# A two-layer hybrid encoder trunk on one core: the feed-forward up phase is ordered by a planner in the source, its first two pairs of tiles are interleaved, and the output projection ahead of it runs tile by tile

## The chip, the core and the metric

One core of a Trainium2 chip. The engines named below are PE (matmuls; PEld is its weight load), DVE (vector), ACT (activations), POOL (GpSimd) and SP, which only issues transfers here. The metric is the time of one launch on the device in microseconds (us); lower is better.

## What is computed

Two layers on x of 1024 tokens by 1024 channels, float32. Layer 0 mixes tokens by grouped-query attention, layer 1 by multi-scale pooling; each layer then cross-attends into 256 memory tokens and runs a gated feed-forward part. The change lies where cross-attention ends and the feed-forward part begins:

```python
x = x + memory_cross_attention(...)        # ends in  o @ w_o, 1024 x 1024
x = x + conv_gated_ffn(rmsnorm(x, ffn_norm[i]), ...)

def conv_gated_ffn(h, w_up, conv_w, conv_b, w_down):
    u = h @ w_up                            # 1024 -> 2 * 2816
    up = jnp.pad(u, ((0, 0), (1, 1), (0, 0)))
    u = up[:, :-2] * conv_w[0] + up[:, 1:-1] * conv_w[1] + up[:, 2:] * conv_w[2] + conv_b
    gate, val = u[..., :D_FF], u[..., D_FF:]
    return (jax.nn.silu(gate) * val) @ w_down
```

## The kernel before

Float32 accuracy is had from three matmuls per product. Each operand is split into a rounded high part and a low remainder by `hi_lo` (line 150: ACT writes the high part at L153, DVE the remainder at L154), and `mm3` (lines 230 to 235) multiplies high by high, high by low and low by high. Operands live in 20 slots `R` of 128x2048, handed out whole or by halves, the longest-free one first. Float32 staging tiles `scr` are six buffers of 128x1024. PSUM has two tiles `pA` of 128x1024 and four `pB` of 128x512. The residual stream is eight tiles `X` of 128 tokens by 1024 channels.

**The output projection.** `project` (lines 248 to 273) runs over the two column halves n of w_o, and in each over the eight token tiles t, with 24 matmuls a tile, and adds the result into X (L261). In the second half the RMS norm of a tile follows its add (`first`, L723 and L219; the old X goes to DRAM as `Xd` before the norm overwrites it), and one tile later its transposes (`second`, L718).

**The up-projection by seven products.** For each of the 22 pairs f (a gate block and a value block of 128 columns of w_up) the product of a 2x2 block matrix of weights A by a 2x2 block matrix of transposed tokens B is taken by seven block products in place of eight. The rows of A are gate and value, its columns the lower and upper 512 channels; the columns of B are two groups of four token tiles, here tiles 0 to 3 and 4 to 7. Token side: `seven_into` (lines 706 to 748) makes B11, B21, B22 and the sums T1 = B12 - B11, T2 = B22 - T1, T3 = B22 - B12, T4 = B21 - T2. It takes the differences in the row layout, on DVE and POOL (L733), and transposes every one of the seven operands of each tile pair by itself. T3 and T4 are left to `tail` (lines 743 to 747), after the projection. Weight side: `load` (L771) brings a gate and a value block, each 512 KB with 128 columns a row, into two of four tiles; `sums` (lines 779 to 785) makes S1 to S4 on POOL into the other two; `split` gives the seven operands to `hi_lo`. Each product is 12 matmuls. Products that share a bank accumulate into it after it has been read: bank z takes P1, P6, P7 and P4 in turn, bank y takes P5 and P3, and P2 has a bank of its own; each product's result is read out before the bank's next one, by a copy on ACT (L811, L879, L882, L896) or an add on DVE (L817, L885, L890).

**The loop.** `ffn_main` (lines 831 to 912) runs the pairs one after the other in the order P1, P5, P6, P3, P7, P2 of the next pair, P4, with one split of the next pair after each product. The weights of pair f+2 and their sums follow at the end of pair f. Then come the convolution (`conv`: one ACT pass at L841, two DVE passes at L842 and L843), the gate's SiLU (L887), the product of gate and value (L902) and the store to the DRAM tile `G` (L903). From pair 1 on, the four weight tiles of a pair are tiles of X, which are free once their transposed forms have been split: pair 1 has X4 to X7. The instruction order of this stage is that of the framework's scheduler. After the last pair, `operand` (line 849) brings rows of G and of w_down back and splits them, and `down` (line 914) multiplies in rounds of four f.

Of the kernel before, what the change touches and what calls it, by code (L numbers as in the profile page):

```python
# [10 lines left out]
F32 = mybir.dt.float32  # L11
# [5 lines left out]
P = 128  # L17
# [98 lines left out]

class Kernel:
# [29 lines left out]
    def stat(self, n, name):  # L147
        return self.st.tile([P, n], F32, name=name, bufs=4)

# [472 lines left out]
    def cross(self, i, hT, qT, ws):  # L622
# [19 lines left out]
        def scores(t):  # L642
# [19 lines left out]
            if t % 4 == 3:  # L662
                for h in range(XH):
                    R.put(qT[h, half])

        def turn(t):
            if t % 4 == 0:
                PT[t // 4] = [R.get() for _ in range(4)]
            self.transposed(prs.pop(t), self.put_T(PT[t // 4], t))
# [17 lines left out]
        for t in range(4):  # L687
            scores(t)
# [5 lines left out]
        turn(4)  # L694
        values(0, (2, 3))
        turn(5)
        turn(6)
# [8 lines left out]
    def seven_into(self, X, gain, Xd):  # L706

        nc, R = self.nc, self.R  # L710
        H = {}

        def turn(name, t, src):
            if name not in H:
                H[name] = [R.get(), R.get()]
            p = self.psB().rearrange("p (a b) -> p a b", a=4)
            for k in range(4):
                nc.tensor.transpose(p[:, k, :], src[:, k * P:(k + 1) * P], self.ident)  # L718
            h, l = (R.v(s, 4)[:, :, (t % 4) * P:(t % 4 + 1) * P] for s in H[name])
            self.hi_lo(h, l, p)  # L720

        def first(t):
            nc.sync.dma_start(out=Xd[t * P:(t + 1) * P, :], in_=X[t])  # L723
            self.normed(X[t], gain, X[t])

        def second(t):
            lo, hi = slice(0, 512), slice(512, 1024)
            if t < 4:
                turn("B11", t, X[t][:, lo])
                turn("B21", t, X[t][:, hi])  # L730
                return
            x, y = X[t - 4], X[t]
            sub = lambda e, out, p, q: e.tensor_tensor(out=out, in0=p, in1=q, op=OP.subtract)  # L733
            sub(nc.vector, x[:, lo], y[:, lo], x[:, lo])
            t2 = self.extra
            sub(nc.vector, t2, y[:, hi], x[:, lo])
            sub(nc.gpsimd, y[:, lo], y[:, hi], y[:, lo])
            sub(nc.gpsimd, x[:, hi], x[:, hi], t2)
            turn("B22", t, y[:, hi])
            turn("T1", t, x[:, lo])  # L740
            turn("T2", t, t2)
# [6 lines left out]
        return (first, second), H, tail  # L748

    def ffn(self, i, H, X, Xd):  # L750
        nc, R, a = self.nc, self.R, self.a
# [4 lines left out]
        cp = self.psB()[:, :4 * 2 * NF].rearrange("p (j f) -> p j f", j=4)  # L756
        for j in range(4):
            nc.tensor.transpose(cp[:, j, :], c3[:, j, :], self.ident[:2 * NF, :2 * NF])
        cv = self.cst.tile([P, 4, 2 * NF], F32, name="conv")
        nc.vector.tensor_copy(cv, cp)  # L760
        wu, wd = a["ffn_w_up"][i], a["ffn_w_down"][i]
        G = self.tc.dram_tile([FF, S], F32, name=f"G{i}")
        raws, ops, bank = {}, {}, {}
        spare = []

        def load(f):

            tiles = [spare.pop(0) for _ in range(4)] if spare else [self.scr() for _ in range(4)]
            for j, c in ((0, f), (1, NF + f)):
                src = wu[:, c * P:(c + 1) * P].rearrange("(k p) n -> p k n", p=P)  # L770
                nc.sync.dma_start(out=tiles[j].rearrange("p (k n) -> p k n", k=NK), in_=src)  # L771
            raws[f] = tiles

        def blocks(f):
            g, v, s, u = raws[f]
            return {"A11": g[:, :512], "A12": g[:, 512:], "A21": v[:, :512], "A22": v[:, 512:],
                    "S1": s[:, :512], "S2": s[:, 512:], "S3": u[:, :512], "S4": u[:, 512:]}

        def sums(f):
            b = blocks(f)  # L780
            tt = nc.gpsimd.tensor_tensor
            tt(out=b["S1"], in0=b["A21"], in1=b["A22"], op=OP.add)  # L782
            tt(out=b["S2"], in0=b["S1"], in1=b["A11"], op=OP.subtract)
            tt(out=b["S4"], in0=b["A12"], in1=b["S2"], op=OP.subtract)
            tt(out=b["S3"], in0=b["A11"], in1=b["A21"], op=OP.subtract)

        def halves(h):
            return R.hv(h)[:, :512], R.hv(h)[:, 512:]

        def split(f, name):  # L790
            h = ops[f, name] = R.get_half()
            self.hi_lo(*halves(h), blocks(f)[name])

        def done(f):
            if f:
                spare.extend(raws[f])
            del raws[f]

        def product(f, left, right, out, start):

            ah, al = (x.rearrange("p (k n) -> p k n", k=4) for x in halves(ops[f, left]))
            bh, bl = (R.v(s, 4) for s in H[right])
            for k in range(4):
                self.mm3(out, ah[:, k], al[:, k], bh[:, k], bl[:, k], start and k == 0, k == 3, not start)
            R.put_half(ops.pop((f, left)))

        def p2(f):
            x = self.psB()
            product(f, "A12", "B21", x, True)
            u = bank[f] = {"g": self.scr()}  # L810
            nc.scalar.copy(u["g"][:, :512], x)  # L811

        def p1(f):
            u = bank[f]
            z = u["z"] = self.psB()
            product(f, "A11", "B11", z, True)
            nc.vector.tensor_tensor(out=u["g"][:, :512], in0=z, in1=u["g"][:, :512], op=OP.add)  # L817

        load(0)
        sums(0)  # L820
        for n in ("A12", "A11", "S1", "S2"):
            split(0, n)

        def go():
            p2(0)
            p1(0)

        return go, lambda late, tail: self.ffn_main(H, X, Xd, late, tail, cv, G, wd, spare, load, sums, split, done,
                                                    product, p1, p2, bank)

    def ffn_main(self, H, X, Xd, late, tail, cv, G, wd, spare, load, sums, split, done, product, p1, p2, bank):
        nc, R = self.nc, self.R
        tail()
        for n in ("S4", "S3", "A22"):
            split(0, n)
        done(0)
        spare.extend(X[t] for t in (4, 5, 6, 7, 0, 1, 2, 3))

        def conv(u, f):
            c = self.scr()  # L840
            nc.scalar.activation(c, u, AF.Identity, scale=cv[:, 1, f:f + 1], bias=cv[:, 3, f:f + 1])  # L841
            nc.vector.scalar_tensor_tensor(c[:, 1:], u[:, :S - 1], cv[:, 0, f:f + 1], c[:, 1:], op0=OP.mult, op1=OP.add)  # L842
            nc.vector.scalar_tensor_tensor(c[:, :S - 1], u[:, 1:], cv[:, 2, f:f + 1], c[:, :S - 1], op0=OP.mult, op1=OP.add)  # L843
            return c

        rounds = [list(range(f, min(f + 4, NF))) for f in range(0, NF, 4)]
        hl = {}

        def operand(kind, f):

            raw = self.scr()
            nc.sync.dma_start(out=raw, in_=(G if kind == "g" else wd)[f * P:(f + 1) * P, :])
            hs = hl[kind, f] = [R.get_half(), R.get_half()]
            self.hi_lo(R.hv(hs[0]), R.hv(hs[1]), raw)

        first = [(kind, f) for f in rounds[0] for kind in ("g", "d")]
        order = ("A12", "A11", "S1", "S2", "S4", "S3", "A22")
        load(1)
        sums(1)
        for f in range(NF):  # L860
            u, left = bank[f], list(order)

            def ahead(n=1):
                for _ in range(n):
                    if f + 1 < NF:
                        if left:
                            split(f + 1, left.pop(0))
                            if not left:
                                done(f + 1)
                    elif first:  # L870
                        operand(*first.pop(0))
# [274 lines left out]
```

## Time and profile before

| | |
|---|---|
| median of 3 runs | 2660.0 us (2659.31 to 2660.57) |
| the profiled execution, its own time | 2661.13 us |
| its span, first to last instruction | 2659.4 us |
| granted TensorE clock, mean | 0.992 |
| HBM read and written | 166.42 MB and 35.65 MB |

The span is what the trace shows; the execution's own time has 1.7 us more around it. In the trace layer 0's output projection runs from about 845 to 949 us, its up phase to about 1381 us and its down phase to about 1600 us; in layer 1 the same stretches lie at about 1875 to 1978, to 2410 and to 2630 us. "PE busy" counts a matmul from its start to its modelled end; since matmuls overlap, what a stage costs is read better from the number of matmuls in a window and the distance between their starts.

### The profile page before, as it was taken

The numbers are of one execution on the slowest core, as the hardware profiler recorded it, in microseconds if no ns is written. First come the engines' busy times: TensorE is split into PE (matmuls) and PEld (weight loads), VectorE is DVE, ScalarE is ACT, GpSimd is POOL, SyncE is SP. The second block draws the span as 40 slices with busy tenths as digits, with TensorE's granted clock in tenths as the row PEclk, the third lists the DMA queues.
The fourth block names the chain that finished last, engine by engine and source line by source line (L and its number), as shares of the span: only waits on it lengthen the run. The fifth ranks groups of instructions, "written<-read, shape, count | busy, mean of one in ns | idle before, by whom it ended". The sixth has DMA issues, their size and how long they took to land.

```text
span 2659.4 us, 36296 instructions
## 1 busy us (share of the span) xinstructions
PE 2595.0 (98%) x13913; PEld 2216.8 (83%) x13913; DVE 1720.5 (65%) x2291; ACT 1207.8 (45%) x2024; POOL 695.0 (26%) x709
## 2 busy tenths in 40 slices
PE   8989999999999999999999998999999999999998
PEld 7988888888898878888878888889878888887886
DVE  6779999955246387777765435425378777767434
ACT  4448888843135255454542205425245555444111
POOL 3664445521012153433300001102034333310001
PEclk9999999999999999999999999999999999999999
DMA  4200000032222132223254203322122232326201
GB/s 157 83 1 1 1 1 1 2 135 65 70 80 89 48 95 73 94 72 95 87 187 154 100 19 89 103 64 72 58 92 91 72 95 72 95 104 241 99 24 63
DMA packets 167554, 209.22 MB, mean 79 GB/s; under 512 B 6741, under 2 KB 134077, under 8 KB 167381
## 3 DMA queue, kind: packets, MB, share of 16 engines
q1 hardware_dynamic: 167381, 206.91, 23.4%
q8 instruction: 109, 1.79, 0.3%
q14 instruction: 64, 0.52, 0.1%
HBM read 166.42 MB, written 35.65 MB: 76 GB/s over the span
## 4 chain that ended last, share of the span: by engine, by line
PE 57%; DVE 2%; ACT 2%; DMA 1%; issue 1%; POOL 1%; SPq 0%; POOLq 0%; DVEq 0%; ACTq 0%
PE pB L234 18%; PE pB L233 18%; PE pB L235 18%; DVE R L154 1%; ACT R L153 1%; DMA scr<-X 0%; DMA scr<-G 0%; PE pA L998 0%; PE pA L233 0%; PE pA L234 0%; PE pA L235 0%; DVE scr L842 0%; PE pB L718 0%; POOL ms L206 0%; DVE scr L843 0%
## 5 line engine op out<-in xcount | busy, mean ns | idle before, releaser
L233 PE MATMUL pB<-R,R 128*128 128x512 f32 (+1 forms) x3088 | 1160.9, 377 | 16.5 <-ACT scr L879 9.6
L234 PE MATMUL pB<-R,R 128*128 128x512 f32 (+1 forms) x3088 | 1157.6, 375 | 4.3 <-DVE R L154 4.0
L235 PE MATMUL pB<-R,R 128*128 128x512 f32 (+1 forms) x3008 | 1125.6, 374 | 0.0
L233 PEld LDWEIGHTS pB<-R,R 128*128 128x128 f32 x3088 | 582.1, 189 | 127.6 <-ACT scr L879 10.4
L234 PEld LDWEIGHTS pB<-R,R 128*128 128x128 f32 x3088 | 582.7, 189 | 109.0 <-DVE R L154 7.5
L235 PEld LDWEIGHTS pB<-R,R 128*128 128x128 f32 x3008 | 567.5, 189 | 101.0 <-DVE R L154 0.4
L153 ACT ACTIVATE R<-scr 128x1024 fp32r<-128x1024 f32 (+1 forms) x186 | 185.7, 1024 | 353.0 <-PE pB L234 283.5
L154 DVE TENSOR_TENSOR R<-X,R 128x512 fp32r<-128x512 f32 x294 | 256.3, 885 | 63.6 <-ACT R L153 63.0
L153 ACT ACTIVATE R<-X 128x512 fp32r<-128x512 f32 x294 | 181.3, 630 | 245.4 <-PE pB L234 225.6
L922 DVE TENSOR_TENSOR X<-pB,X 128x512 f32<-128x512 f32 x192 | 130.9, 688 | 221.3 <-PE pB L235 221.2
L206 POOL TENSOR_SCALAR ms<-ss 128x1 f32<-128x1 f32 (+2 forms) x102 | 26.8, 263 | 909.0 <-ACT scr L214 422.4
L154 DVE TENSOR_TENSOR R<-scr,R 128x1024 fp32r<-128x1024 f32 (+1 forms) x186 | 218.0, 1194 | 49.5 <-ACT R L153 46.2
L153 ACT ACTIVATE R<-pB 128x512 fp32r<-128x512 f32 (+1 forms) x216 | 113.8, 556 | 185.3 <-PE pB L235 81.3
L227 PE MATMUL pB<-ident,scr 128*128 128x128 f32 x1376 | 182.4, 276 | 9.7 <-DVE scr L219 8.0
L227 PEld LDWEIGHTS pB<-ident,scr 128*128 128x128 f32 x1376 | 157.5, 142 | 36.5 <-POOL scr L319 14.6
L319 POOL TENSOR_SCALAR scr<-scr,inv 128x1024 f32<-128x1024 f32 x128 | 144.0, 1125 | 167.2 <-DVE inv L318 162.3
L154 DVE TENSOR_TENSOR R<-pB,R 128x512 fp32r<-128x512 f32 (+1 forms) x216 | 131.4, 636 | 76.9 <-ACT R L153 76.3
L842 DVE SCALAR_TENSOR_TENSOR scr<-scr,conv 128x1023 f32<-128x1023 f32 x88 | 139.4, 1584 | 62.4 <-ACT scr L841 62.0
L782 POOL TENSOR_TENSOR X<-X 128x512 f32<-128x512 f32 x42 | 56.2, 1339 | 447.0 <-DMA X<-in_ffn_w_up 447.0
L154 DVE TENSOR_TENSOR PT<-pB,PT 128x512 fp32r<-128x512 f32 x256 | 163.9, 680 | 3.3 <-ACT PT L153 2.4
L316 ACT ACTIVATE scr<-pA,nm 128x1024 f32<-128x1024 f32 x128 | 142.9, 1116 | 44.6 <-DVE nm L313 42.6
L313 DVE TENSOR_REDUCE nm<-pA 128x1 f32<-128x1024 f32 x128 | 156.1, 1220 | 0.9 <-PE pA L309 0.5
(123 smaller groups left out, 3188.7 us busy)
## 6 DMA issues: line engine op xcount, KB each, us to landing
X<-in_ffn_w_up SPq DMA_DIRECT2D x84, 512.0 KB
G<-scr SPq DMA_DIRECT2D x44, 512.0 KB
scr<-G SPq DMA_DIRECT2D x44, 512.0 KB
scr<-in_ffn_w_down SPq DMA_DIRECT2D x44, 512.0 KB
scr<-in_xattn_w_kv SPq DMA_DIRECT2D x32, 512.0 KB
scr<-in_attn_w_qkv SPq DMA_DIRECT2D x20, 512.0 KB
scr<-in_xattn_w_q SPq DMA_DIRECT2D x16, 512.0 KB
scr<-in_xattn_w_o SPq DMA_DIRECT2D x16, 512.0 KB
```

The lines of the kernel that those rows point to most:

```text
L153: nc.scalar.activation(hi, src, AF.Copy)
L154: nc.vector.tensor_tensor(out=lo, in0=src, in1=hi.bitcast(F32), op=OP.subtract)
L227: self.nc.tensor.transpose(p[:, k, :], src[:, b * P:(b + 1) * P], self.ident)
L233: mm(out, ah, bh, start=start, stop=False)
L234: mm(out, ah, bl, start=False, stop=False)
L235: mm(out, al, bh, start=False, stop=stop)
L313: nc.vector.tensor_reduce(nm, s, axis=AX.X, op=OP.max, negate=True)
L316: nc.scalar.activation(pr, s, AF.Exp, bias=nm, accum_out=rs)
L319: nc.gpsimd.tensor_scalar(pr, pr, ri, 1.0, op0=OP.mult, op1=OP.mult)
L782: tt(out=b["S1"], in0=b["A21"], in1=b["A22"], op=OP.add)
L842: nc.vector.scalar_tensor_tensor(c[:, 1:], u[:, :S - 1], cv[:, 0, f:f + 1], c[:, 1:], op0=OP.mult, op1=OP.add)
L922: nc.vector.tensor_tensor(out=x, in0=p, in1=x, op=OP.add)
```

## The change

- **Projection.** `project` is no longer used here. `ffn` loads the split weights of both column halves ahead; `Seven.begin` runs 16 steps (n, t) in a written order, even token tiles first, so that a tile has both halves after few steps. Even tiles 0, 2, 4, 6 are normed and transposed first, then 1, 3, 5; tile 7's transposes stand between the first up products.
- **Token groups.** The two groups are now the even and the odd tiles. To that end the cross-attention takes its query tiles in the order 0, 2, 4, 6, 1, 3, 5, 7.
- **Transposes.** Each tile of X is transposed once (8 of 128x128). The differences T1 to T4 are taken after that, in the transposed layout, on DVE (two of them a layer on POOL). ACT copies transposed banks back to X for it.
- **Weight sums.** S1 to S4 move from POOL to DVE.
- **First two pairs.** Their products are interleaved, pair 0 and pair 1 by turns; P2 goes to a `pA` tile. The results of a product are written to `scr` with the two token groups interleaved in blocks of 128 columns.
- **Order.** From the first product of the up phase to the operands of the first down round, the kernel records operations with `Plan.add` and `Plan.run` emits them in the order of a list schedule: PE's order is fixed, the other engines take what can begin first, with a preference for the earlier due date; due dates are worked back from PE's order with costs written in `KINDS`; rooms of `scr`, `pA`, `pB` and half slots are counted. The framework's scheduler keeps this order.
- By count, over the whole program: PE has 96 transposes fewer (224 to 128) and as many matmuls; DVE 188 instructions more; POOL 188 fewer; ACT 24 more; SP as many.

```diff
+class Plan:
+    KINDS = {"product": ("PE", 2.72, 2.92), "turn": ("PE", 0.87, 1.07), "add": ("DVE", 0.60, 0.72),
+             "add2": ("DVE", 1.14, 1.25), "tap": ("DVE", 1.20, 1.31), "copy": ("ACT", 0.51, 0.65),
+             "copy2": ("ACT", 0.96, 1.10), "centre": ("ACT", 1.15, 1.28), "silu": ("ACT", 0.96, 1.10),
+             "load": ("SP", 0.40, 4.20), "store": ("SP", 0.40, 4.20)}
+    AHEAD = 30.0
...
+    def run(self):
+        pools = self.pools
+        for op in reversed(self.ops):
+            for o in op["after"]:
+                o["due"] = min(o["due"], op["due"] - o["lag"])
...
+            return t if op["engine"] == "PE" else max(t, op["due"] - self.AHEAD)
...
+                t0 = min(t for t, _ in found)
+                t, op = min((f for f in found if f[0] <= t0 + 0.01), key=lambda f: f[1]["due"])
...
+class Seven:
...
+    def turn(self, t):
+        self.ps[t] = [self.kn.psB() for _ in range(2)]
+        for b in range(NK):
+            self.nc.tensor.transpose(self.ps[t][b // 4][:, b % 4 * P:(b % 4 + 1) * P],
+                                     self.X[t][:, b * P:(b + 1) * P], self.kn.ident)
...
+    def take1(self, t):
+        nc, ps, lo, hi = self.nc, self.ps[t], self.LO, self.HI
+        x, y = self.X[t - t % 2], self.X[t]
+        nc.scalar.copy(y[:, lo], ps[0])
+        if t % 2:
+            self.sub(nc.vector, x[:, lo], ps[0], x[:, lo])
+            self.sub(nc.vector, y[:, hi], ps[1], x[:, lo])
+            self.sub(nc.vector, y[:, lo], ps[1], y[:, lo])
...
+    def sum(self, f, name):
+        p, q, op = self.SUMS[name]
+        self.nc.vector.tensor_tensor(out=self.block(f, name), in0=self.block(f, p), in1=self.block(f, q), op=op)
...
+    def begin(self, gemm, add, free, between):
+        steps = ((0, 0), (0, 2), (1, 0), (1, 2), (0, 4), (1, 4), (0, 6), (1, 6),
+                 (0, 1), (1, 1), (0, 3), (1, 3), (0, 5), (0, 7), (1, 5), (1, 7))
+        turns = {3: 0, 4: 2, 6: 4, 8: 6, 10: 1, 12: 3, 15: 5}
...
+        for i, (n, t) in enumerate(steps):
+            gemm(n, t)
+            free(n, t)
+            u = turns.get(i)
+            if u is not None:
+                self.turn(u)
+            extras.get(i, lambda: None)()
+            add(n, t)
+            if n:
+                self.rows(t)
+            if u is not None:
+                self.take1(u)
+            if n:
+                self.norm(t)
+            if u is not None:
+                self.take2(u)
...
-        def sums(f):
-            tt = nc.gpsimd.tensor_tensor
-            tt(out=b["S1"], in0=b["A21"], in1=b["A22"], op=OP.add)
...
-        def tail():
-            for t in range(4, NT):
-                turn("T3", t, X[t][:, :512])
-            for t in range(4, NT):
-                turn("T4", t, X[t - 4][:, 512:])
...
+            plan = Plan({"DVE": 6.5, "ACT": 4.9}, {"scr": 2, "A": 2, "B": 4, "half": len(R.freed)})
+            places = {1: (1, 3, 5), 0: (7, 0, 2, 4), 2: (6, 1, 3, 5)}
+            order = [(2, 0), (1, 0), None, (2, 1), (1, 1), (5, 0), (5, 1), (3, 0), (3, 1), (6, 0), (6, 1), (7, 0), (7, 1),
+                     (4, 0), (2, 2), (4, 1)]
+            for f in range(2, NF):
+                order += [(1, f), (5, f), (6, f), (3, f), (7, f)] + ([(2, f + 1)] if f + 1 < NF else []) + [(4, f)]
...
+            for f in rounds[0]:
+                for kind in "dg":
+                    plan_operand(plan, kind, f, late)
+                    late += 0.3
...
-        for t in range(4):
-            scores(4 + t)
-            turn(t)
+        for t in range(4):
+            scores(2 * t + 1)
+            turn(2 * t)
```

In `order` an item (n, f) is product Pn of pair f, and None stands for the rest of the token side (tile 7's transposes, T2, T3 and T4 of the odd tiles) and the loads, sums and splits of pair 1.

More of the change, by code (lines that the diff above doesn't have):

```diff
@@ L703, in cross, with conv_table @@
         return O
[L706 to L741, printed above, removed]
-        def tail():
-            for t in range(4, NT):
-                turn("T3", t, X[t][:, :512])
-            for t in range(4, NT):
-                turn("T4", t, X[t - 4][:, 512:])
-        return (first, second), H, tail
-    def ffn(self, i, H, X, Xd):
-        nc, R, a = self.nc, self.R, self.a
+    def conv_table(self, i):
+        nc, a = self.nc, self.a
         cw = self.scr()
@@ L763, in ffn @@
[L763 to L777, printed above, removed]
@@ L794, in done @@
[L794 to L811, printed above, removed]
@@ L813, in p1 @@
[L813 to L829, printed above, removed]
@@ new lines, in turn, with ffn, gemm, add @@
+        def turn():
+            cp = self.psB()[:, :4 * 2 * NF].rearrange("p (j f) -> p j f", j=4)
+            for j in range(4):
+                nc.tensor.transpose(cp[:, j, :], c3[:, j, :], self.ident[:2 * NF, :2 * NF])
+            self.cv = self.cst.tile([P, 4, 2 * NF], F32, name="conv")
+            nc.vector.tensor_copy(self.cv, cp)
+        return turn
+    def ffn(self, i, w, lhs, X, free, late):
+        nc, R, a = self.nc, self.R, self.a
+        Xd = self.tc.dram_tile([S, D], F32, name=f"Xd{i}")
+        U = Seven(self, a["ffn_w_up"][i], lambda f: (f * P, (NF + f) * P), X, Xd, self.bcast(a["ffn_norm"][i]))
+        def gemm(n, t):
+            ps[t] = self.psB()
+            for k in range(NK):
+                self.mm3(ps[t], *lhs(t, k), *self.blk(ws[n], k, slice(0, 512)), k == 0, k == NK - 1)
+        def add(n, t):
+            x = X[t][:, n * 512:(n + 1) * 512]
+            nc.vector.tensor_tensor(out=x, in0=ps.pop(t), in1=x, op=OP.add)
+        def freed(n, t):
+            if t == NT - 1:
+                R.put(*ws[n])
+            if n:
+                free(t)
+        ps = {}
+        ws = [self.load_rows(w, n) for n in range(2)]
+        return self.ffn_main(i, U, X, Xd, late, partial(U.begin, gemm, add, freed, self.conv_table(i)))
@@ L1059, in run @@
         X = [xp.tile([P, D], F32, name=f"X{t}") for t in range(NT)]
-        self.extra = xp.tile([P, 512], F32, name="extra")
         for t in range(NT):
@@ L1100, in late @@
                     ready["pool"] = self.pool_weights()
-            rest, done = ready["ffn"](late, tail)
+            rest, done = self.ffn(i, a["xattn_w_o"][i], lhs, X, free, late)
             if i == 0:
```

447 lines of the change are left out of this document (342 added, 105 removed).

## The prediction

> **What bounds the kernel now.** I read the page's busy times first, then a table of windows, then what PE waited for in the windows that are not full.
>
> ```profile
> span 2659.4 us, 36296 instructions
> PE 2595.0 (98%) x13913; PEld 2216.8 (83%) x13913; DVE 1720.5 (65%) x2291; ACT 1207.8 (45%) x2024; POOL 695.0 (26%) x709
> ```
>
> PE is the bound: 64 us of the span are free of matmuls. Where they are is told by the windows (start:end, length, then each engine's busy time and count, the granted clock, DMA share, GB/s):
>
> ```profile
> 948.00:976.00 28.00, 21.66 (x101) 17.02 (x100) 25.21 (x27) 14.54 (x25) 17.90 (x12) 0.88 0.48 132
> 976.00:1360.00 384.00, 383.99 (x1692) 316.78 (x1691) 288.20 (x298) 192.79 (x279) 129.06 (x75) 1.00 0.27 88
> 1360.00:1392.00 32.00, 30.25 (x131) 24.02 (x130) 24.31 (x23) 16.99 (x18) 0.00 (x0) 1.00 0.60 204
> 1977.00:2006.00 29.00, 22.33 (x107) 17.35 (x106) 26.08 (x27) 15.16 (x27) 19.48 (x13) 0.94 0.44 127
> 2390.00:2422.00 32.00, 29.60 (x128) 23.61 (x127) 25.11 (x25) 16.73 (x19) 0.00 (x0) 1.00 0.62 212
> ```
>
> The second row is the body of layer 0's up phase. It is full, so it gives the true step: 384.00/1692 = 0.227 us from matmul to matmul, 2.72 for a product of 12, 19.07 for a pair of 84. No order of work makes this body shorter. The other rows are where the up phase begins and ends in both layers. In the first and fourth, some of the PE instructions are transposes (L718, here alone), and eight of those take 0.87 us in the chain of waits, 0.109 each:
>
> ```profile
> 948.00:976.00 28.00, 5.70 (x40) 0.88 0.48 132
> 1977.00:2006.00 29.00, 5.83 (x41) 0.94 0.44 127
> 1943.05 0.87 PE pB L718 x8
> ```
>
> Begin, layer 0: 61 x 0.227 + 40 x 0.109 = 18.2 us of work in 28.0, so 9.8 lost. Begin, layer 1: 66 x 0.227 + 41 x 0.109 = 19.5 in 29.0, 9.5 lost. End: 131 x 0.227 = 29.7 in 32.0, 2.3 lost; 128 x 0.227 = 29.1 in 32.0, 2.9 lost. Together 24.5 us. The waits of PE and the chain name the causes (waits of 948 to 976, then of 1360 to 1392; a window of PE alone; the chain of layer 1's begin and of layer 0's end):
>
> ```profile
> PE pB L233 <- ACT scr L879: 4.8, 1, 4.8
> PE pB L233 <- DVE R L154: 0.8, 1, 0.8
> ...
> PE pB L234 <- DVE R L154: 1.3, 1, 1.3
> PE pB L233 <- ACT R L153: 0.5, 1, 0.5
> ...
> 965.00:970.40 5.40, 2.68 (x4) 0.50 0.27 81
> ...
> 1979.98 5.82 DMA X<-in_ffn_w_up
> ...
> 1985.96 1.27 POOL X L782
> ...
> 1367.92 4.94 DMA G<-scr
> ...
> 1372.88 5.62 DMA scr<-G
> ```
>
> At the begin one wait of 4.8 us stands out: the copy that frees a PSUM bank (L879) is queued on ACT behind splits of pair 1, those wait for sums on POOL, and the sums for a load that could start only when X4 to X7 had been split. The window from 965 shows a clock of 0.50 behind that wait: from 965.4 to 970.8 a matmul takes 0.43 us, 12 x 0.20 = 2.4 us more. At the end a store of G and a load of G stand one behind the other, because a staging tile is short, and the splits of the first down operands come late.
>
> **The change part by part.**
>
> *Transposes.* 96 fewer at 0.109 = 10.5 us, all on PE's path. The matmuls are as many as before.
>
> *The begin.* All of the 9.8 and 9.5 us go if the new order keeps PE fed. I follow it from the first up product, P2 of pair 0, at T = 0. The rows:
>
> ```profile
> 948.64 1.89 DVE L154 TENSOR_TENSOR R<-pB,R 128x512 fp32r<-128x512 f32 x3 [0.30 <-ACT R L153]
> 963.84 7.17 DVE L154 TENSOR_TENSOR R<-X,R 128x512 fp32r<-128x512 f32 x5
> L733 DVE TENSOR_TENSOR X<-X,X 128x512 f32<-128x512 f32 x8 | 5.5, 690 | 0.2
> L783 POOL TENSOR_TENSOR X<-X,X 128x512 f32<-128x512 f32 x42 | 83.2, 1981 | 0.0
> L219 DVE SCALAR_TENSOR_TENSOR X<-X,rs,scr 128x1024 f32<-128x1024 f32 x16 | 20.5, 1282 | 8.9 <-DMA Xd<-X 8.7
> L153 ACT ACTIVATE R<-X 128x512 fp32r<-128x512 f32 x294 | 181.3, 630 | 245.4 <-PE pB L234 225.6
> ```
>
> Three half-width DVE instructions in a row take 1.89, so one starts about 0.60 after the other. The five at 963.84 took 1.43 each: POOL's sums ran beside them. POOL's sums, 2 us each, are now 0.69 on DVE (L733 is the same form), and with them the slowing goes. The last gemm of the projection (24 x 0.227 = 5.45) and tile 5's transposes (0.96 with the change of form) end at T. DVE adds tile 7's second half, takes three differences, norms tile 7 (1.28) and does two splits; it is through at about T+4.7, the norm at T+3.6 to 3.9, and PE wants tile 7's transposes at T+5.45: 1.5 us to spare. From there DVE has 34 half-width instructions in its order up to the add that reads P6 of pair 0. At 0.60 and with two short waits (0.2 for tile 7's bank, 0.65 for ACT) they end at T+26.0. Then come that add (26.6), the splits of pair 2's first block, a sum, and the add of P6 of pair 1. The splits wait for pair 2's load into X7, issued when DVE has read X7 last (T+22.0); at 4 to 6 us it lands at T+26 to T+28 and the add is done at T+30 to T+31. PE needs it for P7 of pair 1 at 11 x 2.72 + 0.96 = T+30.9. The next tight place is P6 of pair 2 at T+47.3, whose bank DVE has read by T+46.9. Elsewhere I find over 1 us. So nothing must be lost, but two places have under 1 us; for both layers I take 1 us for them, between 0 and 6 (3 a layer, below).
>
> *Same cover, more work.* While PE does a pair, DVE did and will do this:
>
> ```profile
> L842 DVE SCALAR_TENSOR_TENSOR scr<-scr,conv 128x1023 f32<-128x1023 f32 x40 | 63.9, 1598 | 25.9 <-ACT scr L841 25.6
> L902 DVE TENSOR_TENSOR scr<-scr 128x1024 f32<-128x1024 f32 x20 | 24.4, 1218 | 0.0
> L885 DVE TENSOR_TENSOR scr<-pB,scr 128x512 f32<-128x512 f32 x20 | 13.8, 692 | 35.5 <-PE pB L235 35.5
> 1362.55 1.29 DVE scr L842
> ```
>
> Before: 288.2/384 x 19.07 = 14.3 us. After: 14 half-width instructions (7 splits, 4 sums, 3 adds) at 0.69, four taps at 1.29 (L842 with POOL quiet) and the gate at 1.22, 16.0 us of 19.07; at the pitch of 0.60 less. ACT keeps its instructions, 192.8/384 x 19.07 = 9.6 us. So the four sums a pair cost nothing: PE hides them. Without that cover they would cost 4 x 0.60 = 2.4 us a pair. The adds and copies now write blocks of 128 with gaps; no row has that write, and I take the plain 0.69 of L885, with the 0.60 pitch and twice that as bounds; doubled, the three adds bring DVE to 18.1 us, still under 19.07.
>
> *The end.* The 2.3 and 2.9 us go if the first operands of the down phase come earlier. In SP's new order the w_down and G rows are issued from one pair before the last product, each when a staging tile comes free, and the last two stores of G stand behind loads. By DVE's order, with 1.22 for a full-width split and 5.6 for a load, the last of the eight remainders is done about 1.5 us before PE's first down group needs it; 1.5 us spare for eight loads that share the queue is little. I take 0.5 us a layer as left, between 0 and 2.9.
>
> *The projection.* Its 16 gemms have the same 24 matmuls. Each norm waits for the store of the old X (the 8.7 us of L219 are 0.5 a tile) and had one gemm of 5.45 us for it; it has the same in the new order. The second half of w_o is split earlier, beside cross-attention's last matmuls; SP issues it in the same place as before, so I charge nothing (half a microsecond either way).
>
> Sum: 24.5 + 10.5 - 1.0 (begins) - 1.0 (ends) = 33.0 us. The profiled execution took 2661.1, 1.1 over the median, with a span of 2659.4; taken from the span that is 2626.4, from the execution 2628.1, and from the median 2627.0, which I give.
>
> [...]
>
> **The rivals.**
>
> *DVE late in the first two pairs.* If successive DVE instructions cost 0.69 and not 0.60, the 34 end 3.1 us later and P7 of pair 1 waits some 2 to 3 us; so does P6 of pair 2. For: the order is tight there by the above, and dependent sums cannot overlap. Against: the row with 1.89 for three. About 3 us a layer in place of 0.5: 2632.
>
> *The end stays as it is.* One staging tile short, and store and load of G stand in line again: 5.2 us less gained, less the 1.0 already taken: 2631. For: loads still start only as tiles come free. Against: the last stores are issued behind the loads.
>
> *Slower: DVE holds PE up in every pair.* P6 follows P1 in the same bank with one product between, 2.72 us, in which DVE must read P1. The new DVE order is fixed. Where the add stands behind two taps and a gate that start with it (2 x 1.29 + 1.22 = 3.8) and takes 0.69, PE waits 3.8 + 0.69 - 2.72 = 1.8 us a pair: 44 x 1.8 = 79 us, 2706. It decides from 33/44 = 0.75 us a pair. Against it: in the order the add stands behind one tap at that place, and DVE has 3 us free a pair.
>
> *Clock falls in each pair.* 2.4 us a fall as at 965; 44 x 2.4 = 106 us, 2733.
>
> *It does not do what it says.* The wait at the begin returns at another operand of pair 1 and the end stays: of 35.0 only the transposes and a few microseconds are left, some 2646; or all of it is lost, 2660.
>
> **How the numbers follow.** Forecast 58%; DVE late 16%; end stays 9%; half of it lost 6%; nothing left 2%; slower by DVE 8%; by the clock 1%. A measurement here tells about 0.2%, 5 us, from no change. Faster: 58 + 16 + 9 + 6 = 89%; same 2%; slower 9%. Range: the low end is the whole 35.0 us and 2 more for what lies outside the four windows and for the step from span to median, 2623; the high end takes in both mild rivals together, 2627 + 4 + 4 and some beyond, 2640. That leaves out about 2 in 10.
>
> **What would show it.** Right: 128 transposes; begin windows of both layers full but for under 1 us, no clock of 0.50 there; no wait for a weight load; DVE half-width splits at 0.69 in place of 0.85 and POOL nearly idle in the up phase; PE waits of the end under 1 us. Wrong: PE waits on DVE some 30 and 47 us after the first up product (first rival); PE waits on a split of G rows (second); many equal waits, 44 of them, on DVE adds out of `pB` (slower); clock under 1.00 between 976 and 1360.

## The result, and the profile after

| | before | after |
|---|---|---|
| median of 4 runs each, same chip | 2659.7 us | 2625.0 us (2624.5 to 2626.5) |
| ratio, with its 95% interval | | 0.987 (0.9853 to 0.9887) |
| the profiled execution, its own time | 2661.13 us | 2624.52 us |
| its span | 2659.4 us | 2622.6 us |

The change gains 34.7 us; 33.0 were forecast. First the page's busy times of the changed kernel, then the same kind of windows as before (start:end, length, busy time and count of PE, PEld, DVE, ACT and POOL, granted clock, DMA share, GB/s). Here layer 0's up phase begins at 940.9 and layer 1's at about 1951.

```profile
span 2622.6 us, 35895 instructions
PE 2573.9 (98%) x13817; PEld 2203.1 (84%) x13817; DVE 1732.5 (66%) x2479; ACT 1222.9 (47%) x2048; POOL 376.2 (14%) x521
```

```profile
940.00:968.00 28.00, 28.00 (x133) 23.05 (x132) 25.91 (x43) 19.37 (x36) 0.74 (x2) 1.00 0.21 64
968.00:996.00 28.00, 27.82 (x123) 22.79 (x122) 26.78 (x35) 19.30 (x28) 0.00 (x0) 1.00 0.39 125
996.00:1340.00 344.00, 344.00 (x1519) 284.64 (x1518) 269.73 (x347) 175.04 (x252) 0.00 (x0) 1.00 0.30 84
1340.00:1372.00 32.00, 32.00 (x141) 26.23 (x141) 27.04 (x27) 19.44 (x22) 0.00 (x0) 1.00 0.71 245
1951.00:1987.00 36.00, 36.00 (x165) 29.67 (x164) 33.34 (x52) 26.09 (x45) 0.74 (x2) 1.00 0.30 88
1987.00:2010.00 23.00, 22.69 (x101) 18.50 (x100) 22.34 (x30) 13.83 (x20) 0.00 (x0) 1.00 0.35 115
2372.00:2404.00 32.00, 32.00 (x143) 26.50 (x142) 26.80 (x29) 15.53 (x15) 0.00 (x0) 1.00 0.91 336
```

Begin and end of the up phase are now as full as its body: 344.00/1519 is 0.226 us a matmul, against 0.227 before, and the end windows hold 141 and 143 in 32.0 us, which is the same. The clock is 1.00 in all rows, and POOL does next to nothing. PE's waits from 940 to 1400, and from 1951 to 2410, are one each (engine, line and what it waited for; total, times, longest):

```profile
PE pB L586 <- DVE scr L357: 0.2, 1, 0.2
...
PE pB L586 <- DVE scr L357: 0.3, 1, 0.3
```

For the experiments one measure is used that leaves the rest of the program out, called the stretch of a layer. In each trace it runs from one and the same matmul near the end of cross-attention (54 matmuls, 12 us, ahead of the output projection's first) to the last matmul of the same layer's feed-forward part; in layer 0 it ends 60 matmuls ahead of that, where the first matmuls of layer 1 come between. So it holds the same matmuls in all kernels, but for the transposes. The rest of the program moves by up to 2 us between executions, mostly in the first 800 us; the stretches don't hold that. But each is read from one execution. Against the medians, each less that of the kernel before on its chip, the sums of the table are between 0.3 us lower and 3.6 higher, the 3.6 in pairs_in_turn.

A wait of PE that the text gives is the distance between the starts of two matmuls less the step of 0.227. The lines of waits count from the modelled end of the matmul before and give some 0.16 less.

| kernel | median, us | before on its chip | stretch layer 0 | stretch layer 1 | sum against after |
|---|---|---|---|---|---|
| before | 2659.7 | | 771.6 | 785.2 | +36.2 |
| after | 2625.0 | 2659.7 | 753.7 | 766.8 | 0 |
| before_sums_dve | 2643.4 | 2661.4 | 762.8 | 776.5 | +18.7 |
| sums_on_pool | 2645.8 | 2661.4 | 762.7 | 778.0 | +20.2 |
| pool_shadow | 2652.8 | 2661.1 | 766.8 | 779.8 | +26.1 |
| pool_late | 2633.0 | 2661.1 | 757.5 | 770.7 | +7.7 |
| turn_twice | 2639.5 | 2661.4 | 760.5 | 773.3 | +13.3 |
| pairs_in_turn | 2633.8 | 2661.4 | 760.0 | 771.1 | +10.6 |
| no_due | 2658.4 | 2661.1 | 771.0 | 782.9 | +33.3 |
| operands_late | 2633.4 | 2661.1 | 758.0 | 771.2 | +8.6 |
| hold4 | 2631.6 | 2660.7 | 757.6 | 770.5 | +7.6 |
| hold9 | 2642.1 | 2660.7 | 762.3 | 774.0 | +15.8 |
| dve4 | 2626.3 | 2660.7 | 754.0 | 767.3 | +0.8 |
| dve8 | 2627.8 | 2660.7 | 754.5 | 769.0 | +3.0 |

### The profile page after: what moved, and what is told of

Read it like the earlier page. It is cut to its first block, busy times and chain, and to the rows that moved or that the text cites. A ratio compares the mean times of both kernels' runs of the same rounds, so it can differ in the third digit from the quotient of the medians.

```text
span 2622.6 us, 35895 instructions
## 1 busy us (share of the span) xinstructions
PE 2573.9 (98%) x13817; PEld 2203.1 (84%) x13817; DVE 1732.5 (66%) x2479; ACT 1222.9 (47%) x2048; POOL 376.2 (14%) x521
## 5 line engine op out<-in xcount | busy, mean ns | idle before, releaser
L586 PE MATMUL pB<-R,R 128*128 128x512 f32 (+1 forms) x2864 | 1071.2, 375 | 3.8 <-ACT R L506 1.9
L587 PE MATMUL pB<-R,R 128*128 128x512 f32 (+1 forms) x2848 | 1061.3, 373 | 1.7 <-DVE R L507 1.4
L588 PE MATMUL pB<-R,R 128*128 128x512 f32 (+1 forms) x2784 | 1035.7, 372 | 0.0
L586 PEld LDWEIGHTS pB<-R,R 128*128 128x128 f32 x2864 | 538.7, 188 | 101.5 <-ACT R L506 3.1
L587 PEld LDWEIGHTS pB<-R,R 128*128 128x128 f32 x2848 | 536.4, 188 | 96.0 <-DVE R L507 4.0
L588 PEld LDWEIGHTS pB<-R,R 128*128 128x128 f32 x2784 | 524.1, 188 | 92.0 <-DVE R L507 0.2
L501 DVE TENSOR_TENSOR R<-X,R 128x512 fp32r<-128x512 f32 x310 | 209.9, 686 | 91.2 <-ACT R L498 91.2
L498 ACT ACTIVATE R<-X 128x512 fp32r<-128x512 f32 x310 | 193.3, 631 | 89.9 <-PE pB L587 71.8
L498 ACT ACTIVATE R<-scr 128x1024 fp32r<-128x1024 f32 (+1 forms) x106 | 100.3, 981 | 246.3 <-PE pB L587 160.7
L355 ACT COPY scr<-pB 128x512 f32<-128x512 f32 x132 | 77.4, 586 | 183.5 <-PE pB L588 182.2
L666 DVE TENSOR_REDUCE nm<-pA 128x1 f32<-128x1024 f32 x128 | 156.1, 1220 | 0.9 <-PE pA L662 0.4
L506 ACT ACTIVATE R<-pB 128x512 fp32r<-128x512 f32 (+1 forms) x182 | 94.4, 551 | 127.4 <-PE pB L588 80.4
L507 DVE TENSOR_TENSOR R<-pB,R 128x512 fp32r<-128x512 f32 (+1 forms) x182 | 108.6, 627 | 65.1 <-ACT R L506 64.8
L662 PE MATMUL pA<-R,R 128*128 128x512 f32 x512 | 146.6, 408 | 0.0
L506 ACT ACTIVATE PT<-pB 128x512 fp32r<-128x512 f32 x256 | 138.7, 596 | 13.1 <-PE pB L580 10.9
```

Source lines behind the costliest of these rows:

```text
L498: self.nc.scalar.activation(hi, src, AF.Copy)
L501: self.nc.vector.tensor_tensor(out=lo, in0=src, in1=hi.bitcast(F32), op=OP.subtract)
L506: nc.scalar.activation(hi, src, AF.Copy)
L507: nc.vector.tensor_tensor(out=lo, in0=src, in1=hi.bitcast(F32), op=OP.subtract)
L586: mm(out, ah, bh, start=start, stop=False)
L587: mm(out, ah, bl, start=False, stop=False)
```

## The experiments

Unless another kernel is named, each edit is made in the changed kernel. Edits of two or three lines move the line numbers behind them (L586 is then L588, L357 L358 or L359, L501 L503).

**turn_twice: what a transpose costs.**

```diff
     def turn(self, t):
         self.ps[t] = [self.kn.psB() for _ in range(2)]
         for b in range(NK):
             self.nc.tensor.transpose(...)
+        for b in range(NK):
+            self.nc.tensor.transpose(...)
```

> The changed kernel, each of the 16 tiles transposed twice, the second time over the first: 128 transposes more on PE, nothing else. Theory (every transpose lies on PE's path, which is what the term of 10.5 us for 96 of them rests on): 128 x 0.109 = 14.0 us more than the changed kernel's 2625.0, so 2639.0. Rival (transposes lie in waits of PE for the vector engine and are hidden there in part): under 7 us more, at most 2632.

The stretches are 6.7 and 6.5 us longer, together 13.3 for 128 transposes: 0.104 us each, against 0.109 in the working. Some 0.8 us of small waits go with it (in layer 1 the one 48 us behind the first up product falls from 0.5 to 0.2), which is the difference to 14.0. Transposes lie on PE's path; the 96 that the change removes are worth 10 us or a little more.

**before_sums_dve: the sums alone, in the kernel before.**

```diff
         def sums(f):
             b = blocks(f)
-            tt = nc.gpsimd.tensor_tensor
+            tt = nc.vector.tensor_tensor
```

> The kernel before with one edit: the four sums on DVE, order as its scheduler makes it. Theory (the lost time at the begin needs both: the sums and the load of pair 1's weights, 5.8 us, that waits for four tiles): the wait of 4.8 us falls by the 1.3 to 2 us of one POOL sum and DVE's splits run at 0.69, the rest stays: 2 to 5 us a layer better, 2650 to 2656. Rival A (POOL alone is the cause): the 4.8 us and the half clock behind it go in both layers, 2660 - 14 = 2646 or less. Rival B (the load is the cause): 2658 to 2660.

The theory fell and rival A came out: 8.8 and 8.7 us less, 17.5 of the 19.3 that were lost at the begins, by one word. PE's waits of this kernel from 948 to 1400; the 4.8 us are gone. Of what is left, the 1.0 and 0.8 us lie at the end of the up phase, which this edit doesn't touch, and the 0.6 and 0.2 at its begin:

```profile
PE pB L234 <- DVE R L154: 1.0, 1, 1.0
PE pB L233 <- DVE scr L890: 0.8, 1, 0.8
PE pB L718 <- DVE R L154: 0.6, 1, 0.6
PE pB L233 <- DVE R L154: 0.2, 1, 0.2
```

The load into X4 to X7, which the prediction names as the head of that chain, is as late as it was: its last part is issued at 954.05 here and at 953.65 in the kernel before, and the first sum starts at 956.85 and 956.81. Behind it the two kernels part. DVE and POOL of the kernel before, then DVE of this one, in order of time (start, length, instruction; x6 are six in a row):

```profile
957.06 1.59 DVE L154 TENSOR_TENSOR R<-X,R 128x512 fp32r<-128x512 f32 x1
958.57 0.68 DVE L154 TENSOR_TENSOR R<-pB,R 128x512 fp32r<-128x512 f32 x1
959.17 9.56 DVE L154 TENSOR_TENSOR R<-X,R 128x512 fp32r<-128x512 f32 x6
...
956.81 1.28 POOL L782 TENSOR_TENSOR X<-X 128x512 f32<-128x512 f32 x1 [6.80 <-DMA X<-in_ffn_w_up]
958.06 1.74 POOL L785 TENSOR_TENSOR X<-X,X 128x512 f32<-128x512 f32 x1
959.76 1.71 POOL L783 TENSOR_TENSOR X<-X,X 128x512 f32<-128x512 f32 x1
961.55 1.59 POOL L784 TENSOR_TENSOR X<-X,X 128x512 f32<-128x512 f32 x1
```

```profile
956.85 0.68 DVE L782 TENSOR_TENSOR X<-X 128x512 f32<-128x512 f32 x1
957.45 0.68 DVE L154 TENSOR_TENSOR R<-pB,R 128x512 fp32r<-128x512 f32 x1
958.05 0.68 DVE L783 TENSOR_TENSOR X<-X,X 128x512 f32<-128x512 f32 x1
958.65 0.68 DVE L785 TENSOR_TENSOR X<-X,X 128x512 f32<-128x512 f32 x1
959.25 0.69 DVE L784 TENSOR_TENSOR X<-X,X 128x512 f32<-128x512 f32 x1
959.86 3.09 DVE L154 TENSOR_TENSOR R<-X,R 128x512 fp32r<-128x512 f32 x5
```

Six splits took 9.56 us beside POOL, 1.6 each; five took 3.09 without it, 0.6 each, and the four sums had taken 2.4 us of DVE before them. The split that reads PSUM took 0.68 in both. So DVE was through with sums and five splits at 962.9, where the kernel before was in its fourth split.

**sums_on_pool: the same step undone in the changed kernel.**

```diff
-        self.nc.vector.tensor_tensor(out=self.block(f, name), ...)
+        self.nc.gpsimd.tensor_tensor(out=self.block(f, name), ...)
```

> The changed kernel with the four weight sums of every pair on POOL again, the written order of the other engines as it is. Theory (POOL's sums, 2 us each and slowing DVE beside them, were the cause of the lost time at the begin): the four sums of pair 1 take 8 us in line in place of 2.4, DVE's splits beside them 1.4 in place of 0.69, so the add ahead of P7 of pair 1, which has 0.3 us to spare, comes 4 to 7 us late and the clock may fall behind that wait (2.4 us): 4 to 9 us a layer, 2633 to 2643, and no loss from pair 3 on. Rival (the interleaved order alone did it, sums may stay on POOL): within 2 us, 2625 to 2627.

20 us come back, more than the 8 to 18 expected, and not at one place: in layer 0 PE waits 0.9 us at 975, 3.4 at 990, 1.0 at 1004, 1.4 at 1013, 0.7 at 1026 and 1.1 at 1035, nearly all of them for the adds that read PSUM banks on DVE; from there to 1340 nothing. Waits of this kernel from 940 to 1400:

```profile
PE pB L586 <- DVE scr L357: 6.2, 5, 3.2
PE pB L586 <- ACT R L498: 1.3, 1, 1.3
```

The expectation looked only at the add ahead of P7 of pair 1 and let the loss end with pair 2; every pair whose DVE work isn't yet done ahead loses again.

**pool_shadow: is it POOL's length or its company?** The sums stay on DVE; POOL makes the same sums besides, for nobody.

```diff
     def sum(self, f, name):
         p, q, op = self.SUMS[name]
+        self.nc.gpsimd.tensor_tensor(out=self.kn.spare, in0=self.block(f, p)[:, :448], in1=self.block(f, q)[:, :448], op=op)
         self.nc.vector.tensor_tensor(out=self.block(f, name), ...)
```

> The changed kernel with the sums on DVE as they are, and beside each of them a sum of the same two blocks on POOL (448 of 512 columns) into a spare tile that nobody reads. It tells apart why the sums on POOL cost 20 us. Theory A (POOL slows DVE beside it): DVE's half-width instructions take 1.4 in place of 0.69 while POOL runs, 8 us a pair, some 4 us of DVE for each of the first pairs, about half of the loss comes back: 2632 to 2640. Theory B (each sum on POOL takes 2 us in place of 0.6 and S2 and S4 wait for the one before): DVE's instructions may be longer but PE loses little, 2625 to 2628.

26 us are lost, with no sum that anybody waits for on POOL: theory A, and more of it than half. DVE's groups of this kernel from 970 to 1040 (count, busy us, mean ns of one), then of the changed kernel in the same window:

```profile
L503 DVE TENSOR_TENSOR R<-X,R 128x512 fp32r<-128x512 f32 x32 | 27.2, 876 | 1.8 <-ACT R L500 1.7
L1117 DVE SCALAR_TENSOR_TENSOR scr<-scr,conv 128x1023 f32<-128x1023 f32 x8 | 11.9, 1485 | 0.8 <-ACT scr L1112 0.8
...
L358 DVE TENSOR_TENSOR scr<-pB,scr 128x512 f32<-128x512 f32 x10 | 6.8, 681 | 0.3 <-PE pB L590 0.3
```

```profile
L501 DVE TENSOR_TENSOR R<-X,R 128x512 fp32r<-128x512 f32 x31 | 20.6, 681 | 3.2 <-ACT R L498 3.2
L1115 DVE SCALAR_TENSOR_TENSOR scr<-scr,conv 128x1023 f32<-128x1023 f32 x9 | 11.5, 1277 | 1.9 <-ACT scr L1110 1.9
```

The splits, with both inputs in SBUF, took 876 ns in the mean in place of 681 and the first taps 1485 in place of 1277; the add with one input in PSUM (L358) took 681, as in the changed kernel. Not every group with both inputs in SBUF is longer: the three products of gate and value in this window took 1220, against 1216. That POOL slows DVE is enough for a loss of this size; that POOL's own length adds to it where the sums are really there is likely and wasn't separated. A part of the 26 us may be that the reloading of a weight tile also waits for POOL's read here (one wait of 2.5 us in SP's queue). The rows of the kernel before, above, show the same beside POOL's sums: 1.59 us for a split from SBUF, 0.68 for the one from PSUM.

**pool_late: the sums on POOL where there is time.**

```diff
-        self.nc.vector.tensor_tensor(out=self.block(f, name), ...)
+        (self.nc.gpsimd if f > 4 else self.nc.vector).tensor_tensor(out=self.block(f, name), ...)
```

> The changed kernel with the sums on POOL from pair 5 on, on DVE for pairs 0 to 4. Theory (only the begin is short of time; from pair 5 on the sums of a pair are done some 15 us before its first product): no loss, 2624 to 2628. Rival (POOL beside DVE holds PE up in the body too): 0.5 us or more in each of 34 pairs, 2642 or more.

Between the two: 3.8 and 3.9 us a layer are lost, and they aren't spread over the pairs. The windows of layer 0 show where:

```profile
1000.00:1048.00 48.00, 45.63 (x199) 36.87 (x198) 41.79 (x43) 25.14 (x37) 21.86 (x12) 1.00 0.27 78
1048.00:1340.00 292.00, 292.00 (x1289) 241.64 (x1289) 226.15 (x230) 146.59 (x212) 98.06 (x56) 1.00 0.29 80
```

From 1048 on PE is full although POOL works a third of the time and DVE's splits take 0.92 (x106) in place of 0.69. The loss lies in three waits from 1008 to 1031 (1.0, 0.7 and 1.1 us), where PE is at pairs 3 and 4 and POOL makes the first sums of its own, those of pairs 5 and 6. DVE was then not yet far ahead: in the changed kernel the last sum of a pair starts 2.5 us before the pair's first product for pair 3, 11.5 for pair 4, 14.8 for pair 5 and 15.4 from pair 6 on. The theory's "from pair 5 on" was too early; by these distances one or two pairs later would do, which wasn't run.

**pairs_in_turn: without the interleaving.**

```diff
-            order = [(2, 0), (1, 0), None, (2, 1), (1, 1), (5, 0), (5, 1), (3, 0), (3, 1), (6, 0), (6, 1), (7, 0), (7, 1),
-                     (4, 0), (2, 2), (4, 1)]
-            for f in range(2, NF):
+            order = [(2, 0), (1, 0), None, (5, 0), (6, 0), (3, 0), (7, 0), (2, 1), (4, 0)]
+            for f in range(1, NF):
```

> The changed kernel with the first two pairs one after the other in place of interleaved; the planner works out the order of the other engines anew. Theory (interleaving buys time for the token side): P5 of pair 0 follows P1 of pair 0 at once, 5.4 us earlier, while T1 of tile 7 can be ready some 2 us after the tile's transposes, and P4 of pair 0 wants all of T4 at T+20, up to where DVE has about 24 half-width instructions from T+6.4 (14.4 us, so T+21): waits of 4 to 8 us a layer, 2633 to 2641. Rival (sums on DVE and the freed tiles alone fill the begin): within 2 us, 2625 to 2627.

10.6 us, as expected, but the begin has only half of it: 1.2 and 0.5 us of wait ahead of P5 and inside it, as the expectation has it, and 1.0 at 972; in layer 1 1.4, 0.5 and 1.0. So interleaving is worth some 2.8 us a layer. The rest, 2.1 us of wait at 1368 with slow matmuls behind it (clock 0.59 from 1371 to 1375) and 1.2 us in layer 1, lies at the end of the up phase: the planner made another order there too, and the end has little to spare (below). By the medians the whole loss is 7.0 us, so in other executions the part at the end may be smaller.

**no_due: a planner without due dates.**

```diff
-                t, op = min((f for f in found if f[0] <= t0 + 0.01), key=lambda f: f[1]["due"])
-                for u, other in sorted(found, key=lambda f: f[1]["due"]):
+                t, op = min((f for f in found if f[0] <= t0 + 0.01), key=lambda f: f[1]["at"])
+                for u, other in ():
```

("at" is the place in which an operation was recorded.)

> The changed kernel whose planner takes what can begin first and, of those, what was recorded first, in place of the earlier due date. Theory (due dates matter only where DVE has no time to spare, that is in the first two pairs; in the body DVE has 4 us a pair free and works 15 us ahead): 1 to 8 us a layer, all in the first 60 us of the up phase, 2627 to 2641. Rival A (readiness alone orders it as well): 2625 to 2627. Rival B (adds behind taps in every pair): 1 us or more a pair, over 2660.

Nearly the whole gain is lost, 17.2 and 16.1 us a layer, all but 1 us of it in the first 30 us of the up phase, at one product:

```profile
PE pA L588 <- DVE R L501: 7.8, 1, 7.8
PE pA L586 <- ACT R L498: 6.4, 1, 6.4
PE pB L586 <- DVE scr L357: 0.4, 1, 0.4
```

P2 of pair 1 waits for the split of its operand, high part (ACT) and remainder (DVE), because pair 0's other splits and the token side, recorded earlier, went first (five splits of pair 0 stand in a row on ACT and on DVE at 945 and 947). The place was forecast, the size was not: 14.8 us of waits, and a mean clock of 0.989 over this execution, against 0.995 in the changed kernel's. In the body readiness alone is enough.

**operands_late: the end of the up phase.**

```diff
-            late = 0.0
+            late = 15.0
             for f in rounds[0]:
                 for kind in "dg":
                     plan_operand(plan, kind, f, late)
```

> The changed kernel with the due dates of the first down operands 15 us later, so that the planner issues their loads and splits later; nothing else. Theory (the loss at the end of the up phase is set by when these operands are ready): the eighth remainder is done 4.6 us before PE wants it in the trace, so up to 10.4 us of wait a layer, with the clock falling behind it: 2632 to 2650, PE waiting for splits of G or w_down rows. Rival (the operands were not what PE waited for, other work of DVE was): at most 2 us more, 2627.

4.2 and 4.4 us a layer, of which 3.6 and 3.4 are waits of PE at the end (three in each layer); layer 0's of this window:

```profile
PE pB L586 <- ACT R L498: 1.8, 2, 1.5
PE pB L586 <- DVE X L1239: 1.3, 1, 1.3
```

The mechanism is right: PE waits for the operands' splits and, once a layer (1.5 and 2.2 us), for a bank whose add into X is late because of them. The 4.6 us to spare in the expectation is a miscount. In the changed kernel the last two remainders end at 1362.18 (first row below). The first down group has four of its 12 matmuls ahead of the last up product and eight behind it, and its last, at 1364.30, is the one that reads the last remainder: some 2 us to spare (2.0 in layer 1).

```profile
1359.69 2.50 DVE L501 TENSOR_TENSOR R<-scr,R 128x1024 fp32r<-128x1024 f32 x2
...
1364.30 0.39 PE L588 MATMUL pB<-R,R 128*128 128x512 f32 x1
```

With the edit the eighth remainder ends at 1374.30, 12.1 us later, but only 4.2 arrive. The planner doesn't order the down phase, and its matmuls stand in another order here: in layer 0 four groups begin with the rows that are there, and their last matmuls follow one another within 0.7 us from 1374.70 on. The first add into X comes at 1376.37 in place of 1364.73, and three more follow in 3 us.

**hold4 and hold9: the tight place at T+31, and the clock.** DVE is held straight ahead of one add by instructions that change nothing.

```diff
         else:
+            for _ in range(4 if (f, n) == (1, 6) else 0):
+                self.nc.vector.tensor_tensor(out=out, in0=out, in1=out, op=OP.max)
             self.nc.vector.tensor_tensor(out=out, in0=p, in1=out, op=OP.add)
```

> The changed kernel with four more half-width DVE instructions (a tile compared with itself, result unchanged) straight ahead of the add that reads P6 of pair 1, once a layer. Theory (this add is the tight place at T+31 that the prediction names, with 0.3 us to spare in the trace): 4 x 0.60 - 0.3 = 2.1 us of wait of PE a layer ahead of P7 of pair 1, and the small wait at T+47 stays or goes: 3.6 to 4.8 us more, 2628.6 to 2629.8. Rival (the place has time to spare that the trace does not show, or what follows takes it up): under 1 us.

> The same with nine. Theory (a wait of PE of about 5 us lets the clock fall to 0.50 for the next 12 matmuls, 2.4 us, as it did behind the 4.8 us wait of before): 9 x 0.60 - 0.3 = 5.1 of wait and 2.4 of slow matmuls a layer, 15 us, 2640. Rival (the half clock of before had another cause than the wait): 10.2 us, 2635, and a clock of 1.00 behind it.

The place is right: in layer 0 PE waits once, 3.1 us with four and 6.4 with nine, ahead of P7 of pair 1. Four cost 3.0 us and not 2.4: each reads and writes the tile of the one before, and they start 0.72 apart, against 0.60 for the independent ones above. The rest is a load that landed 0.45 us later in this execution. The clock falls behind both (0.50 in hold4 from 976.40 to 979.20); a window of hold9 in the wait and one behind it (PE busy and count, clock):

```profile
971.20:977.60 6.40, 0.19 (x1) 0.92 0.16 46
977.60:983.30 5.70, 5.66 (x13) 0.50 0.00 0
```

Twelve matmuls at 0.43 us behind the wait, as in the kernel before at 965: the 2.4 us of slow clock there belong to the wait. In layer 1 six are slow behind 6.2 us, where the kernel before has eight. With four added instructions five matmuls are slow, in both layers.

**dve4 and dve8: how much DVE has free.**

```diff
-                    U.plan_left(plan, f, U.SUMS, names)
+                    U.plan_left(plan, f, [*U.SUMS] * (3 if 2 < f < NF - 1 else 1), names)
```

(3 for dve8, 2 for dve4.)

> The changed kernel with each of the four weight sums of pairs 3 to 20 taken twice (same result), known to the planner: 2.4 us more of DVE a pair at the pitch of 0.60. Theory (PE hides DVE's work: DVE is idle 4.1 of 19.07 us a pair): no loss, 2624 to 2627. Rival (DVE's idle time lies between dependent instructions and cannot be used, so PE waits in every pair): 1 us or more a pair, 2660 or more.

> The same with the sums taken three times: 8 x 0.60 = 4.8 us more against 4.1 idle. Theory (DVE's price is its pitch of 0.60 and its idle time can be filled): over by 0.7 us in 36 pairs, some 25 us, 2635 to 2655. Rival A (the price is the duration, 0.69): 5.5 - 4.1 = 1.4 us a pair, 50 us, 2675. Rival B (part of the idle time cannot be filled): beyond that, up to 100 us.

dve4 as expected: 0.8 us. dve8 loses 3.0 us in all, far less than any of the three cases. The same window of the body, dve8 and the changed kernel:

```profile
1060.00:1320.00 260.00, 260.00 (x1149) 215.52 (x1148) 260.00 (x366) 132.09 (x193) 0.00 (x0) 1.00 0.26 83
```

```profile
1060.00:1320.00 260.00, 260.00 (x1149) 215.29 (x1148) 202.56 (x259) 132.61 (x192) 0.00 (x0) 1.00 0.29 81
```

In dve8 both engines are full, and no PE instruction is lost: DVE has just as much work as PE. By pitch, 22 half-width instructions at 0.60, four taps at 1.20 and the gate at 1.14 make 19.1 us a pair, and PE needs 19.07. The busy time that gave 4.1 us free counts the tails that the next instruction overlaps (0.08 of each 0.69); by pitch 4.7 are free, and eight instructions of 0.60 fill them to the end.

## Why the prediction was right, point by point

*What bounds.* Right: what could be had lay in the windows ahead of and behind the body and in the transposes; the body stayed at 0.226 us a matmul. The stretches shrink by 17.9 and 18.3 us, 36.2 together; windows and transposes gave 35.0.

*Transposes, 10.5.* Right, 10 or a little more by turn_twice.

*Begin, 19.3 to be had, 18.3 forecast.* Came: of 19.3 some 0.8 are left, 0.3 and 0.5 us of wait. Both tight places were where the working put them. T is 940.90, and the add that reads P6 of pair 1 ran at T+30.0 to T+30.6, behind a wait for pair 2's load. P7 starts at T+31.2, and in hold4 its first matmul follows the end of that add by 0.14, so some 0.4 us were to spare. A tile's transposes with the change of form, 0.96 in the working, take 0.88 in both traces (946.23 to 947.56 in the changed kernel, less two steps). P6 of pair 2 came 0.3 us late at T+47.8, for the add that reads P1. DVE in the changed kernel, then PE:

```profile
970.25 0.69 DVE L311 TENSOR_TENSOR X<-X 128x512 f32<-128x512 f32 x1 [0.56 <-DMA X<-in_ffn_w_up]
970.86 0.68 DVE L357 TENSOR_TENSOR scr<-pB,scr 128x512 f32<-128x512 f32 x1
...
940.90 0.48 PE L586 MATMUL pA<-R,R 128*128 128x512 f32 x1
...
988.73 0.47 PE L586 MATMUL pB<-R,R 128*128 128x512 f32 x1 [0.17 <-DVE scr L357]
```

Its account of the cause was too long by one step. The prediction led the 4.8 us back over POOL's sums to the load of pair 1's weights. The load is as late in before_sums_dve, where the wait is gone; the sums on POOL, and DVE's splits slowed beside them, were the cause.

*What of the change did it.* The sums on DVE alone are worth 17.5 of the 36.2 us, transposes 10, the ends 5.2. The 5.2 are read from the windows; no run undoes that part alone. By subtraction interleaving and due dates bring about 1 us more than the sums at the begin. But the changed kernel needs them where it is now: without the one it loses some 2.8 us a layer there, without the other 16 to 17. Some 2.5 us aren't assigned. The projection's new order and the new token groups weren't undone by themselves, so what they bring beyond the transposes stays open.

*Same cover, more work.* Right: the four sums a pair on DVE cost nothing in the body, four more cost 0.8 us in all, and eight more 3.0. The writes with gaps, which no row of before had, take 685 ns (L357), the value taken.

*End, 5.2 to be had, 4.2 forecast.* All of it came; the 1.5 us to spare that the working gave are some 2 in the trace.

*The size.* 33.0 forecast against 34.7 for the medians. The two terms of 1.0 for what would be left of begins and ends were mis-sized: 0.8 and nothing.

*The rivals.* DVE late in the first two pairs: the price of an instruction is its pitch, 0.60, as dve8 shows (0.72 where one depends on the one before, in hold4), so the 34 weren't late; hold4 shows what 3 us of lateness there would have cost, 3.8 us a layer. The end stays: no, but it is some 2 us from it. DVE holds PE up in each pair: no wait of PE between 996 and 1340. Clock falls in each pair: 1.00 in every row of the windows of the changed kernel above.

## What to carry to other kernels

Before moving work to an idle engine, read what it does to its neighbour: in the kernel before, POOL's sums of two SBUF blocks more than doubled DVE's splits beside them (1.6 us each against 0.6), and moving the sums onto the *busier* engine gave 17.5 us by one word. Price DVE work by the distance between starts (0.60 here), not by duration (0.69), and fill only what that leaves. Extra time on a helping engine cost nothing here where the stage had run for some pairs and was far ahead (pool_late, no wait of PE from 1048 to 1340), and showed at once where the stage begins (sums_on_pool, waits of 0.7 to 3.4 us from 975 to 1035): look at the first 60 us of a stage by themselves.

## What the runs showed of the hardware that was not expected

The slow clock behind a wait doesn't follow from the length of that wait alone. In sums_on_pool a wait of 3.41 us in layer 0 left it at 1.00, and one of 3.43 us in layer 1 was followed by 12 matmuls of 0.43 us. A wait of 1.98 us in pool_shadow and one of 2.06 us in pairs_in_turn were followed by 7 slow matmuls each, starting over 1 us after PE had gone on; one of 2.21 us in operands_late by none. In the kernel before, waits of 1.3 and 0.5 us between 1360 and 1392 left it at 1.00. What else decides it, no run here shows.
